# Linear ReLU attention on one core: K, V and Q prepared an octet ahead, first loads in whole rows, two stores cut by partitions

## The chip, the core and the metric

The kernel runs on one core of a Trainium2 chip. Its time is device microseconds (us), here of the one core. The profile comes from one profiled execution. The engines are PE (matmul) with its weight loads (PEld), DVE (vector), ACT (scalar), POOL (GpSimd) and SP (which only issues transfers). DMA transfers are issued by SP, ACT and POOL.

## The reference

```python
batch, heads, seq, dim = 8, 12, 512, 64          # Q, K, V: float32
Q_feat = np.maximum(0, Q)
K_feat = np.maximum(0, K)
KV = np.einsum('bhkd,bhkv->bhdv', K_feat, V)
K_sum = np.sum(K_feat, axis=2)
numerator = np.einsum('bhqd,bhdv->bhqv', Q_feat, KV)
denominator = np.einsum('bhqd,bhd->bhq', Q_feat, K_sum)
return (numerator / (denominator[:, :, :, None] + 1e-10)).astype(np.float32)
```

There are 96 heads of 512 rows of 64 numbers. Each of Q, K, V and the output is 12.58 MB of float32.

## The kernel before

Heads are taken in groups of four for K and V (24 groups `g`) and in octets of eight for Q and the output (12 octets `o`; octet `o` holds groups `2o` and `2o+1`). A tile has 128 partitions; a partition holds 16 consecutive rows of K or V (4 KB of float32) or 32 rows of Q or of the output (8 KB). So the 32 partitions of one head lie together.

**Loads.** Groups 0 and 1 are loaded as float32 by SP (K, L99) and ACT (V, L100), each tensor in two halves of 8 rows, 2 KB per partition. They borrow two buffers of the output pool (`kv_first`). Everything else is loaded by POOL, which turns float32 into bfloat16 on the way: Q of octet 0, and then per octet K, V, K, V, Q (`load_kv`, `load_q`; L85, L87, L91). All these loads are issued in program order from the start and run ahead as far as the pools (`kin` and `vin` 12 buffers, `qin` 7) and the outstanding transfers permit.

**Preparation of a group.** `prep` makes on DVE two copies of relu(K), one masked to the even heads and one to the odd (L130), and a copy of V masked to one half of the partitions (L132). `prep_act` makes on ACT the copy of V masked to the other half (L136). Beside V stands a column of ones, which yields the sum of K. The buffers are `kf` (pool `kfp`, 3) and `vo` (`NB`, 3).

**Products.** `mm_kv` makes 16 matmuls on PE (L141) that sum K times V over the rows of four heads. `evac_kv` copies the result by four ACT instructions into `kvd` (L148), laid out for two heads at a time.

**Q.** `transp` transposes Q by 16 matmuls with an identity, in two halves of eight (L155), and `evac_qt` takes the relu by two ACT instructions per half (L161) into `qtz` (two buffers).

**Output.** `mm_out` makes numerators and denominators of an octet in three rounds of 48, 48 and 32 matmuls (L176); `norm` adds 1e-10, takes the reciprocal and multiplies, on DVE (L186, L188, L189), into `o_sb`. `store` issues the transfer to HBM from SP (L204). Ahead of the store of each octet `o` below 7, SP reads a few bytes of K of octet `o+5` into `scratch` (L199). That read waits for the landing of that K, so it holds back the store, and all later ones, until loads five octets ahead have landed (`DELAY = 5`). The stores of octets 7 to 11 are issued in two halves of 16 rows, 4 KB per partition.

The order of all work is written out by hand; each engine takes its instructions in the order of the program. The loop runs over octets, and the outputs lag by one: pass `o` makes the products of group `2o`, prepares `2o+1`, makes two output rounds of octet `o-1`, the products of `2o+1`, the DVE part of the preparation of `2o+2`, the third round and the store of `o-1`, the transposes of Q of octet `o`, and at last `prep_act` of `2o+2`.

Of the kernel before, what the change touches and what calls it, by code (L numbers as in the profile page):

```python
# [10 lines left out]
def kernel(  # L11
# [7 lines left out]
    nc = tc.nc  # L19
    B, H, S, D = Q.shape  # L20
    assert D == 64
    P = 128
# [4 lines left out]
    R = S * 4 // P  # L27
    RQ = S * 8 // P
# [3 lines left out]
    NO = NG // 2  # L32
# [4 lines left out]
    fp32 = mybir.dt.float32  # L37
    bf16 = mybir.dt.bfloat16
    Act = mybir.ActivationFunctionType
    Alu = mybir.AluOpType  # L40

    def pool(name, bufs, **kw):
        return ctx.enter_context(tc.tile_pool(name=name, bufs=bufs, **kw))
# [2 lines left out]
    qin = pool("qin", 7)  # L46
    kin = pool("kin", 12)
    vin = pool("vin", 12)
    kfp = pool("kfp", 3)
    rcp = pool("rcp", 4)  # L50
    outp = pool("outp", DELAY + 2)
    pkv = pool("pkv", 2, space=bass.MemoryType.PSUM)
# [3 lines left out]
    def view(X, f):  # L56
        return X.rearrange("b h s d -> (b h s d)").rearrange("(n p f) -> n p f", p=P, f=f)

    Qr, Kr, Vr, Or = view(Q, RQ * D), view(K, R * D), view(V, R * D), view(out, RQ * D)

    ident = consts.tile([P, P], bf16, name="ident")
    NB = 3
    NK = 4
    NZ = 2

# [2 lines left out]

    vo = [consts.tile([P, R, 2, D1], bf16, name=f"vo{i}") for i in range(NB)]
    kvf = [consts.tile([P, NHG * 2 * D1], bf16, name=f"kvd{i}") for i in range(NK)]  # L70
# [6 lines left out]
    qtz = [x.rearrange("p z (u w y c) -> p z u w y c", u=U, w=4, y=2) for x in qtf]  # L77
# [3 lines left out]
    q_sb, k_sb, v_sb = {}, {}, {}  # L81
# [7 lines left out]
    def load_q(o):  # L89
        q_sb[o] = qin.tile([P, U, 2 * D], bf16, name="q_sb")  # L90
        nc.gpsimd.dma_start(out=q_sb[o].rearrange("p u f -> p (u f)"), in_=Qr[o])  # L91


    for g in range(F32):
        kv = outp.tile([P, 2, R, D], fp32, name="kv_first", tag="o_sb")
        k_sb[g], v_sb[g] = kv[:, 0], kv[:, 1]
        for i in range(2):
            rs, fs = slice(R // 2 * i, R // 2 * (i + 1)), slice(R // 2 * D * i, R // 2 * D * (i + 1))
            nc.sync.dma_start(out=k_sb[g][:, rs].rearrange("p r d -> p (r d)"), in_=Kr[g][:, fs])  # L99
            nc.scalar.dma_start(out=v_sb[g][:, rs].rearrange("p r d -> p (r d)"), in_=Vr[g][:, fs])  # L100
    load_q(0)
    make_identity(nc, ident)
    for o in range(1, NO):
# [4 lines left out]
    def zero(i):  # L108
        if i == 0:
            for h in range(NHG):  # L110
                for s in range(2):
                    nc.vector.memset(mask[32 * h:32 * h + 32, 0, s:s + 1], 1.0 if h % 2 == s else 0.0)
            for t in range(2):
                nc.vector.memset(mask[:, 1, t:t + 1], 0.0)
                nc.vector.memset(mask[64 * t:64 * t + 64, 1, t:t + 1], 1.0)
        if i < NB:
            nc.vector.memset(vo[i][:, :, :, D:D1], 0.0)
            for t in range(2):
                nc.vector.memset(vo[i][64 * t:64 * t + 64, :, t, D:D1], 1.0)
        nc.vector.memset(kvf[i].bitcast(fp32), 0.0)  # L120

    def zero_q(i):
        nc.vector.memset(qtf[i].rearrange("p z f -> p (z f)").bitcast(fp32), 0.0)  # L123
# [3 lines left out]
    def prep(g):  # L127
        kf[g] = kfp.tile([P, R, 2, D], bf16, name="kf")
        for s in range(2):
            nc.vector.tensor_scalar(kf[g][:, :, s, :], k_sb[g], scalar1=0.0,  # L130
                                    scalar2=mask[:, 0, s:s + 1], op0=Alu.max, op1=Alu.mult)
        nc.vector.tensor_scalar(vo[g % NB][:, :, 0, 0:D], v_sb[g], scalar1=mask[:, 1, 0:1],  # L132
                                scalar2=None, op0=Alu.mult)

    def prep_act(g):
        nc.scalar.activation(vo[g % NB][:, :, 1, 0:D], v_sb[g], Act.Copy, scale=mask[:, 1, 1:2])  # L136

    def mm_kv(g):
        ps_kv[g] = pkv.tile([P, 2, D1], fp32, name="ps_kv")
        for r in range(R):  # L140
            nc.tensor.matmul(  # L141
                ps_kv[g], kf[g][:, r, :, :].rearrange("p s d -> p (s d)"), vo[g % NB][:, r, :, :],
                start=(r == 0), stop=(r == R - 1), skip_group_check=True)

    def evac_kv(g):
        for s in range(2):
            for c in range(2):
                nc.scalar.copy(kvd[g % NK][64 * c:64 * c + 64, :, s, c, :],  # L148
                               ps_kv[g][64 * s:64 * s + 64])


    def transp(o, i):
        ps_qt[o, i] = pqt.tile([P, U // 2, P], bf16, name="ps_qt")
        for u in range(U // 2):
            nc.tensor.transpose(ps_qt[o, i][:, u, :], q_sb[o][:, i * (U // 2) + u, :], ident)  # L155

    def evac_qt(o, i):
        us = slice(i * (U // 2), (i + 1) * (U // 2))
        pv = ps_qt[o, i].rearrange("p u (w y c) -> p u w y c", w=4, y=2)
        for z in range(2):  # L160
            nc.scalar.activation(qtz[o % NZ][:, z, us, :, z, :], pv[:, :, :, z, :], Act.Relu)  # L161


    ROUNDS = ((0, 6), (6, 6), (12, 4))
# [1 line left out]
    def mm_out(o, j):  # L166
        po = pou.tile([P, 2, 512], fp32, name="ps_out")
        ps_out[o, j] = po
        u0, nu = ROUNDS[j]
        for v in range(nu):  # L170
            u, b, c = u0 + v, v // (nu // 2), v % (nu // 2) * 2 * D1
            for z in range(2):
                for w in range(4):
                    hs = slice(32 * w, 32 * w + 32)
                    h = 2 * w + z
                    nc.tensor.matmul(  # L176
                        po[hs, b, c:c + 2 * D1],
                        qtf[o % NZ][:, z, u * P + 32 * w:u * P + 32 * w + 32],
                        kvd[(2 * o + h // 4) % NK][:, h % 4 // 2, h % 2, :, :],
                        start=(z == 0), stop=(z == 1), skip_group_check=True)  # L180

    def norm(o, j, o_sb):
        u0, nu = ROUNDS[j]
        pv = ps_out[o, j][:, :, 0:nu * D1].rearrange("p b (r d) -> p b r d", d=D1)
        den = rcp.tile([P, 2, nu], fp32, name="den")
        nc.vector.tensor_scalar(den, pv[:, :, :, D], scalar1=1e-10, scalar2=None, op0=Alu.add)  # L186
        rec = rcp.tile([P, 2, nu], fp32, name="rec")
        nc.vector.reciprocal(rec, den)  # L188
        nc.vector.tensor_tensor(  # L189
            o_sb[:, 2 * u0:2 * (u0 + nu)].rearrange("p (b r) d -> p b r d", b=2),  # L190
            pv[:, :, :, 0:D],
            rec.unsqueeze(3).to_broadcast([P, 2, nu, D]), op=Alu.mult)

    def store(o, o_sb):
        if o + DELAY < NO:
            nc.sync.dma_start(out=scratch, in_=k_sb[2 * (o + DELAY)][0:1, 0, :])  # L199
        parts = 2 if o >= NO - 5 else 1  # L200
        n = RQ // parts
        for j in range(parts):
            rs = slice(n * j, n * (j + 1))
            nc.sync.dma_start(out=Or[o].rearrange("p (r d) -> p r d", d=D)[:, rs], in_=o_sb[:, rs])  # L204

    zero(0)
    prep(0)
    prep_act(0)
    zero(1)
    zero_q(0)  # L210
    o_sb = {}
    for o in range(NO + 1):
        if o < NO:
            mm_kv(2 * o)
            prep(2 * o + 1)
            prep_act(2 * o + 1)
            evac_kv(2 * o)
        if o == 0:
            for k in range(2, NK):
                zero(k)  # L220
            zero_q(1)
        if o > 0:
            o_sb[o - 1] = outp.tile([P, RQ, D], fp32, name="o_sb", tag="o_sb")
            for j in range(2):
                mm_out(o - 1, j)
                norm(o - 1, j, o_sb[o - 1])
        if o < NO:
            mm_kv(2 * o + 1)
            evac_kv(2 * o + 1)
        if o + 1 < NO:  # L230
            prep(2 * o + 2)
        if o > 0:
            mm_out(o - 1, 2)
            norm(o - 1, 2, o_sb[o - 1])
            store(o - 1, o_sb[o - 1])
        if o < NO:
            for i in range(2):
                transp(o, i)
                evac_qt(o, i)
        if o + 1 < NO:  # L240
            prep_act(2 * o + 2)
# [1 line left out]
_INS = ['Q', 'K', 'V']  # L243
_OUTS = [((8, 12, 512, 64), 'float32')]
# [25 lines left out]
```

## Time and profile before

| | us |
|---|---|
| median of 8 runs | 133.66 |
| lowest, highest | 131.95, 135.38 |
| the profiled execution | 133.41 |
| its span, first to last instruction | 131.6 |
| PE matmul busy | 78.7 |
| PE weight loads busy | 70.2 |
| DVE busy | 79.1 |
| ACT busy | 76.9 |
| POOL busy | 32.6 |

The profile numbers the lines as in the listing above. Its slices cut the span into 40 equal parts of 3.29 us, and each digit is a share in tenths. A share of the DMA engines is the time of the packets of all queues over 16 engines, so it can pass 1 where packets of two queues are under way on one engine together. q0 is the queue of POOL's loads, q1 that of SP, q10 that of ACT. A wait is put down to the instruction or the transfer that released it.

### The profile page before, as it was taken

The numbers are of one execution on the slowest core, as the hardware profiler recorded it, in microseconds if no ns is written. First come the engines' busy times: TensorE is split into PE (matmuls) and PEld (weight loads), VectorE is DVE, ScalarE is ACT, GpSimd is POOL, SyncE is SP. The second block draws the span as 40 slices with busy tenths as digits, with TensorE's granted clock in tenths as the row PEclk, the third lists the DMA queues.
The fourth block names the chain that finished last, engine by engine and source line by source line (L and its number), as shares of the span: only waits on it lengthen the run. The fifth ranks groups of instructions, "written<-read, shape, count | busy, mean of one in ns | idle before, by whom it ended". The sixth has DMA issues, their size and how long they took to land.

```text
span 131.6 us, 4834 instructions
## 1 busy us (share of the span) xinstructions
PE 78.7 (60%) x2112; PEld 70.2 (53%) x2112; DVE 79.1 (60%) x207; ACT 76.9 (58%) x169; POOL 32.6 (25%) x62
## 2 busy tenths in 40 slices
PE   0022283992937929438947839829839739389710
PEld 0032274882937828327937639629729638279510
DVE  2174883395592982860791973943955927908580
ACT  0060669359598297387198593594693694972600
POOL 6802525324343431240240240151230000000000
PEclk9999999999997799985699995995995999968996
DMA  3999999999999999999999999999999999992725
GB/s 103 307 272 275 216 205 214 209 209 215 207 218 205 218 259 312 214 261 313 212 250 332 213 244 331 210 213 326 252 213 326 248 238 376 405 390 118 315 97 230
DMA packets 11909, 32.82 MB, mean 249 GB/s; under 512 B 1520, under 2 KB 1520, under 8 KB 10992
## 3 DMA queue, kind: packets, MB, share of 16 engines
q0 software_dynamic: 8064, 17.83, 70.9%
q1 hardware_dynamic: 3248, 13.63, 26.2%
q10 hardware_dynamic: 576, 1.05, 2.4%
q8 instruction: 16, 0.26, 0.7%
q14 instruction: 5, 0.04, 0.1%
HBM read 37.75 MB, written 12.58 MB: 382 GB/s over the span
## 4 chain that ended last, share of the span: by engine, by line
PE 52%; ACT 23%; DMA 8%; issue 7%; DVE 4%; SPq 1%; ACTq 0%; DVEq 0%
PE ps_out L176 25%; PE ps_kv L141 23%; ACT qt L161 14%; ACT vo L136 9%; DMA kv_first<-in_K_dram 8%; PE ps_qt L155 5%; DVE o_sb L189 2%; SPq L99 1%; DVE kf L130 1%; ACT kvd L148 1%; DVE rec L188 1%; DVE vo L132 1%; ACTq L265 0%; DVE den L186 0%; ACTq L136 0%
## 5 line engine op out<-in xcount | busy, mean ns | idle before, releaser
L141 PE MATMUL ps_kv<-vo,kf 128*128 128x130 bf16 x384 | 32.5, 249 | 43.2 <-ACT vo L136 38.4
L141 PEld LDWEIGHTS <-kf 128*128 128x128 bf16 x384 | 28.6, 112 | 46.3 <-issue 28.3
L148 ACT CAST kvd<-ps_kv 64x130 bf16<-64x130 f32 x96 | 25.3, 263 | 32.8 <-PE ps_kv L141 31.3
L176 PE MATMUL ps_out<-kvd,qt 128*32 128x130 bf16 x1536 | 35.4, 260 | 3.6 <-issue 2.3
L176 PEld LDWEIGHTS <-qt 128*32 128x32 bf16 x1536 | 30.2, 117 | 7.4 <-issue 3.9
L189 DVE TENSOR_TENSOR o_sb<-ps_out,rec 128x768 f32<-128x768 f32 (+1 forms) x36 | 31.3, 868 | 1.4
L186 DVE TENSOR_SCALAR den<-ps_out 128x12 f32<-128x12 f32 (+1 forms) x36 | 5.8, 161 | 37.3 <-PE ps_out L176 37.3
L161 ACT ACTIVATE qt<-ps_qt 128x512 bf16<-128x512 bf16 x48 | 24.9, 602 | 3.4 <-PE ps_qt L155 2.9
L136 ACT ACTIVATE vo<-v_sb,mask 128x1024 bf16<-128x1024 bf16 x22 | 24.7, 1190 | 0.0
L85 POOL DMA_DIRECT2D k_sb<-in_K_dram x22 | 12.5, 570 | 35.5 <-DMA q_sb<-in_Q_dram 22.5
L130 DVE TENSOR_SCALAR kf<-k_sb,mask 128x1024 bf16<-128x1024 bf16 x44 | 19.2, 477 | 0.0
L87 POOL DMA_DIRECT2D v_sb<-in_V_dram x22 | 12.4, 562 | 21.3 <-DMA k_sb<-in_K_dram 10.8
L155 PE MATMUL ps_qt<-ident,q_sb 128*128 128x128 bf16 x192 | 14.0, 227 | 0.7 <-issue 0.6
L155 PEld LDWEIGHTS <-q_sb 128*128 128x128 bf16 x192 | 11.7, 102 | 2.1 <-issue 0.9
L132 DVE TENSOR_SCALAR vo<-v_sb,mask 128x1024 bf16<-128x1024 bf16 x22 | 10.5, 478 | 0.0
L91 POOL DMA_DIRECT2D q_sb<-in_Q_dram x12 | 7.2, 600 | 7.9 <-DMA v_sb<-in_V_dram 5.6
L188 DVE RECIPROCAL rec<-den 128x12 f32<-128x12 f32 (+1 forms) x36 | 7.9, 220 | 1.2
L130 DVE TENSOR_SCALAR kf<-kv_first,mask 128x1024 bf16<-128x1024 f32 x4 | 2.8, 750 | 5.8 <-DMA kv_first<-in_K_dram 5.8
L136 ACT ACTIVATE vo<-kv_first,mask 128x1024 bf16<-128x1024 f32 x2 | 2.4, 1178 | 4.7 <-DMA kv_first<-in_V_dram 4.7
L136 ACT ACT_TABLE_LOAD x1 | 1.3, 1283 | 6.4 <-DMA kv_first<-in_V_dram 6.4
L123 DVE MEMSET qt<- 128x2048 f32 x2 | 3.5, 1765 | 0.8 <-issue 0.8
L132 DVE TENSOR_SCALAR vo<-kv_first,mask 128x1024 bf16<-128x1024 f32 x2 | 1.5, 747 | 0.0
(12 smaller groups left out, 3.2 us busy)
## 6 DMA issues: line engine op xcount, KB each, us to landing
out_dram<-o_sb SPq DMA_DIRECT2D x7, 1024.0 KB, 8.7
q_sb<-in_Q_dram POOLq DMA_DIRECT2D x12, 512.0 KB, 15.4
k_sb<-in_K_dram POOLq DMA_DIRECT2D x22, 256.0 KB, 14.1
v_sb<-in_V_dram POOLq DMA_DIRECT2D x22, 256.0 KB, 13.2
out_dram<-o_sb SPq DMA_DIRECT2D x10, 512.0 KB, 7.7
kv_first<-in_V_dram ACTq DMA_DIRECT2D x4, 256.0 KB, 7.0
kv_first<-in_K_dram SPq DMA_DIRECT2D x4, 256.0 KB, 6.8
scratch<-k_sb SPq DMA_DIRECT2D x7, 0.1 KB, 5.0
```

The source lines that it names most:

```text
L85: nc.gpsimd.dma_start(out=k_sb[g].rearrange("p r d -> p (r d)"), in_=Kr[g])
L87: nc.gpsimd.dma_start(out=v_sb[g].rearrange("p r d -> p (r d)"), in_=Vr[g])
L130: nc.vector.tensor_scalar(kf[g][:, :, s, :], k_sb[g], scalar1=0.0, scalar2=mask[:, 0, s:s + 1], op0=Alu.max, op1=Alu.mult)
L132: nc.vector.tensor_scalar(vo[g % NB][:, :, 0, 0:D], v_sb[g], scalar1=mask[:, 1, 0:1], scalar2=None, op0=Alu.mult)
L136: nc.scalar.activation(vo[g % NB][:, :, 1, 0:D], v_sb[g], Act.Copy, scale=mask[:, 1, 1:2])
L141: nc.tensor.matmul(ps_kv[g], kf[g][:, r, :, :].rearrange("p s d -> p (s d)"), vo[g % NB][:, r, :, :], start=(r == 0), stop=(r == R - 1), s ...
L148: nc.scalar.copy(kvd[g % NK][64 * c:64 * c + 64, :, s, c, :], ps_kv[g][64 * s:64 * s + 64])
L155: nc.tensor.transpose(ps_qt[o, i][:, u, :], q_sb[o][:, i * (U // 2) + u, :], ident)
L161: nc.scalar.activation(qtz[o % NZ][:, z, us, :, z, :], pv[:, :, :, z, :], Act.Relu)
L176: nc.tensor.matmul(po[hs, b, c:c + 2 * D1], qtf[o % NZ][:, z, u * P + 32 * w:u * P + 32 * w + 32], kvd[(2 * o + h // 4) % NK][:, h % 4 // ...
L188: nc.vector.reciprocal(rec, den)
L189: nc.vector.tensor_tensor(o_sb[:, 2 * u0:2 * (u0 + nu)].rearrange("p (b r) d -> p b r d", b=2), pv[:, :, :, 0:D], rec.unsqueeze(3).to_broa ...
```

## The change

It has four parts. K and V of a group are prepared a whole octet before their products, with four buffers for `kf` and `vo` instead of three, and Q of octet `o` is transposed before the third output round of octet `o-1` rather than after it; the loop is written anew for that, with another order at its end. In the last octet the second half of the Q evacuation goes to DVE. The first loads of K and V are one transfer each, with 4 KB per partition. The stores of octets 1 and 3 are issued as five transfers of 112, 5, 5, 5 and 1 partitions, and those of octets 7 to 10 as one transfer instead of two halves.

```diff
-    kfp = pool("kfp", 3)
+    kfp = pool("kfp", 4)
...
-    NB = 3
+    NB = 4
...
-        for i in range(2):
-            rs, fs = slice(R // 2 * i, R // 2 * (i + 1)), slice(R // 2 * D * i, R // 2 * D * (i + 1))
-            nc.sync.dma_start(out=k_sb[g][:, rs].rearrange("p r d -> p (r d)"), in_=Kr[g][:, fs])
-            nc.scalar.dma_start(out=v_sb[g][:, rs].rearrange("p r d -> p (r d)"), in_=Vr[g][:, fs])
+        nc.sync.dma_start(out=k_sb[g].rearrange("p r d -> p (r d)"), in_=Kr[g])
+        nc.scalar.dma_start(out=v_sb[g].rearrange("p r d -> p (r d)"), in_=Vr[g])
...
-    def evac_qt(o, i):
+    def evac_qt(o, i, eng=None):
...
         for z in range(2):
-            nc.scalar.activation(qtz[o % NZ][:, z, us, :, z, :], pv[:, :, :, z, :], Act.Relu)
+            if eng is nc.vector:
+                eng.tensor_scalar(qtz[o % NZ][:, z, us, :, z, :], pv[:, :, :, z, :], scalar1=0.0,
+                                  scalar2=None, op0=Alu.max)
+            else:
+                nc.scalar.activation(qtz[o % NZ][:, z, us, :, z, :], pv[:, :, :, z, :], Act.Relu)
...
+    def cuts(o):
+        return ((16, P), (0, 5), (5, 10), (10, 15), (15, 16)) if o in (1, 3) else ((0, P),)
...
     def store(o, o_sb):
         if o + DELAY < NO:
             nc.sync.dma_start(out=scratch, in_=k_sb[2 * (o + DELAY)][0:1, 0, :])
-        parts = 2 if o >= NO - 5 else 1
-        n = RQ // parts
-        for j in range(parts):
-            rs = slice(n * j, n * (j + 1))
-            nc.sync.dma_start(out=Or[o].rearrange("p (r d) -> p r d", d=D)[:, rs], in_=o_sb[:, rs])
+        Ov = Or[o].rearrange("p (r d) -> p r d", d=D)
+        if o == NO - 1:
+            for j in range(2):
+                rs = slice(RQ // 2 * j, RQ // 2 * (j + 1))
+                nc.sync.dma_start(out=Ov[:, rs], in_=o_sb[:, rs])
+            return
+        for p0, p1 in cuts(o):
+            nc.sync.dma_start(out=Ov[p0:p1], in_=o_sb[p0:p1])

     zero(0)
     prep(0)
     prep_act(0)
     zero(1)
+    prep(1)
+    prep_act(1)
     zero_q(0)
-    o_sb = {}
+    for k in range(2, NK):
+        zero(k)
+    zero_q(1)
+    def kv(g):
+        mm_kv(g)
+        evac_kv(g)
+    def qt(o):
+        for i in range(2):
+            transp(o, i)
+            evac_qt(o, i, nc.vector if o == NO - 1 and i == 1 else None)
+    def prepare(g):
+        prep(g)
+        prep_act(g)
+    def out_round(o, j, o_sb):
+        mm_out(o, j)
+        norm(o, j, o_sb)
     for o in range(NO + 1):
-        if o < NO:
-            mm_kv(2 * o)
-            prep(2 * o + 1)
-            prep_act(2 * o + 1)
-            evac_kv(2 * o)
-        if o == 0:
-            for k in range(2, NK):
-                zero(k)
-            zero_q(1)
-        if o > 0:
-            o_sb[o - 1] = outp.tile([P, RQ, D], fp32, name="o_sb", tag="o_sb")
-            for j in range(2):
-                mm_out(o - 1, j)
-                norm(o - 1, j, o_sb[o - 1])
-        if o < NO:
-            mm_kv(2 * o + 1)
-            evac_kv(2 * o + 1)
-        if o + 1 < NO:
-            prep(2 * o + 2)
-        if o > 0:
-            mm_out(o - 1, 2)
-            norm(o - 1, 2, o_sb[o - 1])
-            store(o - 1, o_sb[o - 1])
-        if o < NO:
-            for i in range(2):
-                transp(o, i)
-                evac_qt(o, i)
-        if o + 1 < NO:
-            prep_act(2 * o + 2)
+        if o > 0:
+            o_sb = outp.tile([P, RQ, D], fp32, name="o_sb", tag="o_sb")
+        if o < NO - 1:
+            kv(2 * o)
+        if o > 0:
+            out_round(o - 1, 0, o_sb)
+        if o < NO - 2:
+            prepare(2 * o + 2)
+        if o > 0:
+            out_round(o - 1, 1, o_sb)
+        if o < NO - 1:
+            kv(2 * o + 1)
+            qt(o)
+        if o < NO - 2:
+            prepare(2 * o + 3)
+        if o > 0:
+            out_round(o - 1, 2, o_sb)
+            store(o - 1, o_sb)
+        if o == NO - 2:
+            prepare(2 * NO - 2)
+        if o == NO - 1:
+            prepare(2 * NO - 1)
+            kv(2 * NO - 2)
+            kv(2 * NO - 1)
+            qt(o)
```

## The prediction

> **What bounds the kernel now.** I read four views in this order: the page's slices and queue shares, the busy time by stretches, the waits, and the last part of the timeline with the landings of single transfers. First the page's head, its DMA rows and its queue shares:
>
> ```profile
> span 131.6 us, 4834 instructions
> ...
> PE 78.7 (60%) x2112; PEld 70.2 (53%) x2112; DVE 79.1 (60%) x207; ACT 76.9 (58%) x169; POOL 32.6 (25%) x62
> ...
> DMA  3999999999999999999999999999999999992725
> ...
> q0 software_dynamic: 8064, 17.83, 70.9%
> q1 hardware_dynamic: 3248, 13.63, 26.2%
> q10 hardware_dynamic: 576, 1.05, 2.4%
> ...
> HBM read 37.75 MB, written 12.58 MB: 382 GB/s over the span
> ```
>
> No engine is busy for more than 60%, but the DMA row is full from slice 1 to slice 35 and has holes only in the last four (118.5 us on). Busy time by stretches puts numbers on it (the last two columns are the DMA engines' share and GB/s written):
>
> ```profile
> 44.00:104.00 60.00, 41.12 (x1124) 36.76 (x1117) 38.72 (x98) 38.73 (x88) 15.47 (x27) 0.86 1.08 263
> 104.00:119.00 15.00, 9.29 (x268) 8.21 (x269) 8.26 (x22) 11.62 (x24) 0.00 (x0) 0.90 1.02 337
> 119.00:131.60 12.60, 5.91 (x232) 4.86 (x224) 7.03 (x17) 3.12 (x8) 0.00 (x0) 0.91 0.47 188
> ```
>
> A share over 1 means that packets of several queues lie on an engine at once: it is saturated. One octet moves 3 x 1.05 MB of fp32 in and 1.05 MB out, 4.19 MB; in steady state one octet's loads land every 10.0 us (the gate reads on SP, each released by a K load, start at 43.9, 53.9, 63.9, 73.9 us), that is 419 GB/s. Only at the end do the DMA engines run dry. The waits, however, show no steady-state compute instruction waiting for a load:
>
> ```profile
> PE ps_kv L141 <- ACT vo L136: 38.4, 12, 8.9
> DVE den L186 <- PE ps_out L176: 37.3, 13, 4.8
> ACT kvd L148 <- PE ps_kv L141: 31.3, 18, 3.1
> ...
> DVE kf L130 <- DMA kv_first<-in_K_dram: 5.8, 2, 3.6
> ```
>
> Compute waits on itself: PE for ACT's copy of V (L136), ACT and DVE for PE. So compute is late on its own account. The last Q load is issued at 97.06 us and lands 16.0 us later, at 113.1; its transposes begin at 121.38. The timeline of the end, PE and SP:
>
> ```profile
> 115.69 1.64 PE L141 MATMUL ps_kv<-vo,kf 128*128 128x130 bf16 x16 [2.76 <-ACT vo L136]
> 117.26 2.56 PE L176 MATMUL ps_out<-kvd,qt 128*32 128x130 bf16 x96
> 119.75 1.11 PE L141 MATMUL ps_kv<-vo,kf 128*128 128x130 bf16 x16
> 120.79 0.65 PE L176 MATMUL ps_out<-kvd,qt 128*32 128x130 bf16 x32
> 121.38 1.07 PE L155 MATMUL ps_qt<-ident,q_sb 128*128 128x128 bf16 x16
> ...
> 121.58 6.61 SPq L204 DMA_DIRECT2D out_dram<-o_sb  x4
> ```
>
> Octet 9's last store is issued at 114.35 and lands 7.2 us later, at 121.5; octet 10's first half is only issued at 121.58, octet 11's last at 127.86, landing at 130.75. Two limits in turn, then: DMA bandwidth until about 120 us, then a compute chain that is 8.3 us behind its loads (121.4 - 113.1) and feeds the last 2.1 MB of stores to idle DMA engines.
>
> **What the Trainium skill says.** "DMA: Bandwidth & Descriptors", Issuing engines are not separate DMA queues: transfers of all queues share the same 16 engines. The trace agrees: q0's share drops while q1 stores, and the sum stays near 1.08. The same page, Why a DMA increments its semaphore by 16: the engine count k is the largest up to 16 that divides the outer sizes, on the lowest-numbered engines. So 112 partitions give 7 rows to each of 16 engines, 5 partitions one row to engines 0 to 4, one partition one row to engine 0 unless it is split. No transfer here has such a shape, so the trace can't confirm it. "TensorE: Matmul & The Clock Gate", Part 1: an idle PE falls to half clock after about 3.4 us and needs as long to recover. The trace agrees in kind: clock 0.86 over 44 to 104 us, and 16 of L141's matmuls take 1.09 us or 1.89.
>
> **The change, part by part.** The sum is made on the profiled execution: span 131.6, time 133.41, so 1.8 us lie outside the span; the median of the runs, 133.66, is 0.25 above it.
>
> *Preparation and transposes ahead.* Instruction counts stay. Before, in each octet, the order is K and V copies, products, Q transposes, evacuation, and ACT's V copy (L136) stands behind four evacuations of 0.6 us (L161): the chain L155, L161, L136, L141 costs 2.5 to 2.8 us of PE time each octet (38.4 us in 12 waits, of which 8.9 is the start). After, L141's inputs are made a loop pass earlier and PE finds them ready. The period was (121.4 - 17.2)/11 = 9.5 us; per octet DVE and ACT are busy some 6.2 to 6.5 us (from 44 to 104 us: 38.7/6) and PE 6.9, so without the stall a period of 7 to 8 us is possible. The loads deliver one octet per 7.5 us before stores begin (Q lands at 19.4, 26.8, 35.2), then per 10. Compute catches up 8.3 us in a few octets and then waits for loads. That wait is what is late next: `prepare` stands between two output rounds on DVE, so rounds of octet o-1 queue behind K and V of octet o+1; those land within 6 us after Q of octet o, and stores wait for K five octets ahead, so nobody who matters waits for them. POOL's queue and the load order stay; loads are paced by bandwidth, not by buffers, so freeing buffers sooner gains nothing.
>
> *What the end becomes.* The two last octets' 2.1 MB now follow without a hole. Octet 9's store halves (4 KB rows) land 1.24 us apart (120.27, 121.51), so a whole octet costs the slowest engine 2.5 us: 121.5 + 2 x 2.5 = 126.5 for the last landing, if stores are issued in time. Are they? With K, V (22, 23) landed at 109.0 and Q at 113.1: `prepare(23)` on DVE behind octet 10's rounds to about 113.2, L141 1.1, transposes 1.07 (to 115.4), evacuations behind L148's four casts to 116.6 (half of them now on DVE beside ACT; a PSUM-source move of its size isn't in the trace, I bound it between ACT's 0.5 and 1.2 us for two and take 1.1), then three rounds at 1.35 on DVE: store halves at about 120.2 and 121.2. Octet 10's store is issued by 114. An unloaded half lands 2.7 to 2.9 us after issue, so the compute path would end at 124.1 at full clock, under 126.5. Half clock would add 0.8 for L141, 0.9 for the transposes and 0.6 for the first round: 126.4. Bandwidth sets the end, with little to spare.
>
> *First loads in 4 KB rows.* Four transfers instead of eight. q10's share, 2.4% of 16 x 131.6 us over 512 data rows, is 99 ns for 2 KB; q1's stores, after taking out 50 us for K's first loads, are 26.2% - 2.4% = 501 us over 12.58 MB, 163 ns for 4 KB. 512 rows of 4 KB x (198 - 163) / 16 engines = 1.1 us at most; queues overlap at the start (share 1.07), so between 0 and 1.1; I take 0.6. The second group should land earlier too (13.3 before), which pulls compute's start forward by 2 to 3 us; loads hide that.
>
> *Stores in cuts.* Octets 1 and 3: engines 5 to 15 write 7 rows instead of 8, engines 0 to 4 ten, engine 0 eleven. One 8 KB row is 2 x 163 = 0.33 us; two fewer are 0.65 on eleven engines, 1.3 to 2.0 more on five. A DMA ends with its slowest engine, and the engines are far apart: for the last Q load the trace has the first of its 16 completion marks at 108.0 and the last at 113.1. No view says which engine is late. Value: -0.65 if it is one of 5 to 15, +1.3 to +2.0 if one of 0 to 4; I take -0.6, eleven of sixteen and an early group of at least five being there to take the load. SP issues eight more transfers at 0.5 us, in the middle of 10 us of waiting. Whole stores for octets 7 to 10 have 8 KB rows instead of 4 KB: nothing, the rate is the same.
>
> *Sum.* 126.5 - 0.6 - 0.6 = 125.3; plus 0.85 from landing to span's end (131.6 - 130.75) = 126.2; I add 0.3 for holes between queues: 126.5. Plus 1.8 outside: 128.3 against 133.41. On the median's level: 128.4, or 3.9% faster.
>
> **Rivals.**
> A. The compute tail sets the end. If PE runs at half clock (for: PE now idles for loads, clock 0.57 from 116 to 120 even before; against: its last octet is dense), or if octet 10's rounds end later than I lay them, store halves come at 123.5 and 124.5: last landing 127.4, time about 130.5 with a late round.
> B. The cuts load the late engines: 128.4 + 0.6 + 1.3 to 2.0 = 130.5.
> C. The reordering doesn't speed compute, a new hand-over between DVE and PE taking L136's place (for: DVE rounds hold PSUM for PE, 37.3 us of waits; against: PE then has two more tasks to go on with). Only the start's gain remains: 132.5 to 134, no change.
> D. Slower: PE at half clock throughout. Then L141 costs 2 x 1.89, L176 2.72 + 1.2, L155 1.9: 9.6 us an octet, and with 0.2 of hand-over 9.8. It decides from a period of 9.6: starting 3 us earlier, the last transposes come at 14.2 + 11 x 9.8 = 122, the slow tail adds 10.2 + 2.3, and with 1.8 outside the time is 136. Against it: before, with PE no busier, the granted clock is 0.90.
>
> **How the numbers follow.** Forecast 0.66, A 0.17, B 0.06, C 0.06, D 0.05. About 1% is what a measurement of this kernel can tell from no change. Faster by over 1%: forecast, A and B, 0.89; within: C, 0.06; slower: D, 0.05. Low end: if the engines end level (the mean of the 16 completion marks of octet 9's last store is 119.7, not 121.5) and the start gives 1.1, the time is 126.3. High end: A and B with a margin, 131.2.
>
> **What would show it.** Right: the DMA row full to the last two slices; few holes after 119 us; DVE or ACT waiting for k_sb, v_sb and PE for q_sb loads; "PE ps_kv <- ACT vo" mostly gone; last Q landing near 112; a span near 126.5. For the first loads: group 1 landed by about 10.5 us. For the cuts: last Q completions closer than 5 us. Wrong: holes after the last Q landing with DMA share below 0.8 (A), a longer load phase (B), an unchanged 8 us between the last Q's landing and its transposes (C), or a mean clock below 0.7 (D).

## The result, and the profile after

The changed kernel takes 127.51 us (median of 11 runs, 127.36 to 127.72); the kernel before, run beside it and earlier, 133.93 (32 runs). The ratio is 0.964, with a 95% interval of 0.961 to 0.967; it compares the fast runs of each kernel alone (the kernel before runs from 131.17 to 135.38 us) and so lies nearer to 1 than the quotient of the medians, 0.952. The forecast was 128.4, 3.9% under the 133.66 that it started from; on that base 127.51 is 4.6% less. The profiled execution took 127.5 us and its span is 125.7.

First the page's head of the kernel after, with the rows shown of before:

```profile
span 125.7 us, 4876 instructions
...
PE 76.6 (61%) x2112; PEld 67.4 (54%) x2112; DVE 81.0 (64%) x212; ACT 76.5 (61%) x167; POOL 31.5 (25%) x62
...
DMA  3999999999999999999999999999999999999994
...
q0 software_dynamic: 8064, 17.83, 74.4%
q1 hardware_dynamic: 2416, 13.63, 27.1%
q10 hardware_dynamic: 288, 1.05, 2.2%
q8 instruction: 16, 0.26, 0.8%
...
HBM read 37.75 MB, written 12.58 MB: 400 GB/s over the span
```

The DMA row now has no hole before its last slice. The engines did the same work in nearly the same busy time (PE 76.6 us for 78.7, DVE 81.0 for 79.1); what is gone are the hollow slices at the end. Busy time by stretches (last two columns: DMA share and GB/s written):

```profile
44.00:104.00 60.00, 41.51 (x1204) 36.42 (x1203) 39.96 (x98) 42.00 (x95) 14.03 (x26) 0.89 1.09 262
104.00:119.00 15.00, 9.31 (x304) 8.12 (x304) 9.53 (x26) 7.11 (x16) 0.00 (x0) 0.89 1.04 360
119.00:125.70 6.70, 0.13 (x12) 0.00 (x0) 1.72 (x4) 0.00 (x0) 0.00 (x0) 0.71 0.69 281
```

After 119 us the DMA share is 0.69 where it was 0.47, and the stretch is 6.7 us long where it was 12.6. The middle moves data at the same rate as before. The waits:

```profile
PE ps_out L178 <- issue: 15.2, 9, 3.3
ACT vo L134 <- DMA v_sb<-in_V_dram: 9.6, 5, 3.9
PE ps_kv L139 <- ACT vo L134: 8.9, 2, 8.1
```

PE's wait for ACT's copy of V (38.4 us in 12 waits before) is down to 8.9 in two, 8.1 of it the start. ACT now waits for loads of V, as it never did in steady state before. And PE's wait "issue" before the output rounds, 2.3 us in two waits before, is 15.2 in nine: it stood still with nothing in this view that it waited for. More of that below. The end on PE and SP:

```profile
111.83 1.92 PE L139 MATMUL ps_kv<-vo,kf 128*128 128x130 bf16 x16 [2.24 <-DVE vo L130]
113.53 1.77 PE L153 MATMUL ps_qt<-ident,q_sb 128*128 128x128 bf16 x16
...
116.12 1.52 PE L178 MATMUL ps_out<-kvd,qt 128*32 128x130 bf16 x92 [0.25 <-ACT qt L163]
...
119.78 1.47 SPq L211 DMA_DIRECT2D out_dram<-o_sb  x2
```

The last Q load is issued at 95.54 us and lands 16.0 later, at 111.5; its transposes begin at 113.5. Compute's lag behind its loads has shrunk from 8.3 us to 2.0. The last two store halves are issued at 119.8 and 120.8 and land at 123.6 and 124.8, 3.8 and 4.0 us after issue; in the kernel before, on idle engines, they took 2.6 and 2.9. The stores queue: the engines set the end, by some 1.1 us.

### The profile page after: what moved, and what is told of

It is laid out like the page before. It is cut to its first block, busy times and chain, and to the rows that moved or that the text cites. A ratio compares the mean times of both kernels' runs of the same rounds, so it can differ in the third digit from the quotient of the medians.

```text
span 125.7 us, 4876 instructions
## 1 busy us (share of the span) xinstructions
PE 76.6 (61%) x2112; PEld 67.4 (54%) x2112; DVE 81.0 (64%) x212; ACT 76.5 (61%) x167; POOL 31.5 (25%) x62
## 3 DMA queue, kind: packets, MB, share of 16 engines
q10 hardware_dynamic: 288, 1.05, 2.2%
## 4 chain that ended last, share of the span: by engine, by line
DMA 32%; PE 30%; issue 14%; DVE 12%; ACT 7%; ACTq 1%; SPq 0%
DMA v_sb<-in_V_dram 25%; PE ps_out L178 14%; PE ps_kv L139 12%; DMA kv_first<-in_K_dram 7%; PE ps_qt L153 3%; ACT kvd L146 3%; DVE o_sb L191 3%; DVE qt L121 3%; ACT qt L163 3%; DVE kf L128 2%; DVE vo L130 2%; ACT vo L134 1%; DVE rec L190 1%; ACTq L294 0%; DVE den L188 0%
## 5 line engine op out<-in xcount | busy, mean ns | idle before, releaser
L178 PE MATMUL ps_out<-kvd,qt 128*32 128x130 bf16 x1536 | 32.8, 238 | 18.9 <-issue 15.2
L139 PEld LDWEIGHTS <-kf 128*128 128x128 bf16 x384 | 27.3, 111 | 24.4 <-DVE vo L130 16.4
L178 PEld LDWEIGHTS <-qt 128*32 128x32 bf16 x1536 | 26.1, 105 | 24.3 <-issue 17.6
L134 ACT ACTIVATE vo<-v_sb,mask 128x1024 bf16<-128x1024 bf16 x22 | 26.1, 1188 | 9.7 <-DMA v_sb<-in_V_dram 9.6
L163 ACT ACTIVATE qt<-ps_qt 128x512 bf16<-128x512 bf16 x46 | 23.9, 602 | 0.5 <-PE ps_qt L153 0.2
L153 PE MATMUL ps_qt<-ident,q_sb 128*128 128x128 bf16 x192 | 16.1, 249 | 2.7 <-issue 2.7
L153 PEld LDWEIGHTS <-q_sb 128*128 128x128 bf16 x192 | 14.5, 115 | 2.8 <-issue 2.8
L91 POOL DMA_DIRECT2D q_sb<-in_Q_dram x12 | 6.5, 542 | 8.4 <-DMA v_sb<-in_V_dram 4.5
L160 DVE TENSOR_SCALAR qt<-ps_qt 128x512 bf16<-128x512 bf16 x2 | 0.8, 418 | 3.6 <-PE ps_qt L153 3.6
```

What stands on the lines that cost most here:

```text
L139: nc.tensor.matmul(ps_kv[g], kf[g][:, r, :, :].rearrange("p s d -> p (s d)"), vo[g % NB][:, r, :, :], start=(r == 0), stop=(r == R - 1), s ...
L178: nc.tensor.matmul(po[hs, b, c:c + 2 * D1], qtf[o % NZ][:, z, u * P + 32 * w:u * P + 32 * w + 32], kvd[(2 * o + h // 4) % NK][:, h % 4 // ...
```

## The experiments

### Two cuts, no cuts, three, five

Edits of the cut function alone:

```diff
 e1_no_cuts
-        return (...five cuts...) if o in (1, 3) else ((0, P),)
+        return ((0, P),)
 e11_three_cuts
+        return (...five cuts...) if o in (1, 3, 5) else ((0, P),)
 e9_five_cuts
+        return (...five cuts...) if o in (0, 1, 2, 3, 4) else ((0, P),)
```

> The changed kernel with the stores of octets 1 and 3 as one transfer each. Theory (the DMA engines set the end and the latest of them are among 5 to 15): each of those gets two 8 KB rows back, 2 x 0.33 us; 127.5 + 0.4 to 0.65 = 127.9 to 128.2, and the last Q load's 16 completion marks spread wider again than the 4.4 us of the changed kernel. Rival 1 (the compute tail sets the end): 127.5. Rival 2 (a late engine is among 0 to 4 and the cuts cost time): 126.5 to 127.0.

> The changed kernel with the stores of octets 1, 3 and 5 cut, three instead of two. Theory (two cuts nearly level the engines, whose last marks lie 1.2 us apart): the eleven win 0.33, the five lose 0.65 and engine 0 1.0; 127.4 to 128.2. Rival (the eleven are still late by more than a row): 127.2.

> The changed kernel with the stores of octets 0 to 4 cut, five instead of two: against two cuts, engines 5 to 15 write three 8 KB rows less (-1.0 us each), engines 0 to 4 six more (+2.0), engine 0 nine more (+2.9). Theory (the five lowest engines were the early ones by about 1.5 to 2.3 us, as the marks without cuts lie apart, and two cuts nearly level them): now these five are late, 124.8 for the last landing becomes about 126 to 127: 128.7 to 129.7. Rival (any row taken from engines 5 to 15 still helps): 127.0 or less. Rival (the engines that get the rows are not the early ones, or the cut only changes something in the middle): 127.5.

Measured: none 128.13 us (127.92 to 128.31), two 127.51 (127.36 to 127.72), three 128.45 (128.29 to 128.59), five 130.45 (130.37 to 130.72). Two cuts bring 0.62, which fits the two rows of 0.33 that eleven engines write less (an 8 KB packet of q1 took 0.32). The expected wider spread for the last Q load without cuts did not show: its marks go from 107.5 to 111.6, 4.1 us, against 4.4. What the cuts moved shows in octet 10's store, which is issued while the engines are full. Without cuts its 16 completion marks fall into two halves, eight at 119.8 to 121.2 us and eight at 122.0 to 122.8. With two cuts three stay early (119.3 to 120.0) and thirteen lie together, at 121.5 to 122.3. The traces of e8_three_buffers and e10_shifted_pe, with two cuts, have the same three and thirteen; that of e3_order_only, with none, the same two halves.

The marks also show how many engines a transfer uses. One of 112 partitions leaves 16. One of 5 partitions leaves five about 8 us after its issue, and one of 1 partition a single one; each has besides a mark half a microsecond after the issue, too early for a landing. So five engines take part in the one and one engine in the other: the single row is not split.

From the third cut on, time rises, and by more than was expected: 0.94 for one more, 2.94 for three more. In the profiled executions the last landing moves from 124.78 us (two cuts) to 125.27 (three) and 127.29 (five). From three to five that is 1.01 per cut: three rows of 0.33 and not the two that engines 0 to 4 have in common. From two to three it is only 0.49; the rest of that execution's 0.82 comes after the last landing. So with five cuts one engine that takes all three small transfers and the single row is the last. Its mark stands alone, 0.5 us after the one before it, where with three cuts the last four marks lie within 0.15 us. By the rule of the Trainium skill ("DMA: Bandwidth & Descriptors", Why a DMA increments its semaphore by 16) that is engine 0; the profile does not name engines. With five cuts the last stretches, DMA share in the column before the last, show the few engines left:

```profile
125.00:126.00 1.00, 0.00 (x0) 0.00 (x0) 0.00 (x0) 0.00 (x0) 0.00 (x0) 0.50 0.41 168
126.00:126.50 0.50, 0.00 (x0) 0.00 (x0) 0.00 (x0) 0.00 (x0) 0.00 (x0) 0.50 0.14 57
126.50:127.00 0.50, 0.00 (x0) 0.00 (x0) 0.00 (x0) 0.00 (x0) 0.00 (x0) 0.50 0.04 16
```

One engine of 16 is a share of 0.06: from 126 us on two are at work on average, from 126.5 on less than one. Two cuts are the best of the four numbers tried.

### First loads in halves, with and without the cuts

```diff
 e2_half_first: K and V of groups 0 and 1
-        nc.sync.dma_start(out=k_sb[g].rearrange(...), in_=Kr[g])
-        nc.scalar.dma_start(out=v_sb[g].rearrange(...), in_=Vr[g])
+        for i in range(2):
+            ...
+            nc.sync.dma_start(out=k_sb[g][:, rs].rearrange(...), in_=Kr[g][:, fs])
+            nc.scalar.dma_start(out=v_sb[g][:, rs].rearrange(...), in_=Vr[g][:, fs])
 e3_order_only: the same, and no cuts
```

> The changed kernel with each first load of K and V in two halves with 2 KB per partition. Theory: the engines lose time in the first 8 us that is never made good, since they are full until the end. In the two profiles Q of octet 1 lands at 19.35 and 18.04, so +1.3: 128.8. By the prediction's own term, +0.6: 128.1. Rival (the start is hidden by later slack): 127.5.

> The changed kernel with both of the two other parts undone: stores of octets 1 and 3 whole, first loads in halves. What is left is the new order of the work with four buffers (and whole stores for octets 7 to 10). Theory: the order closes the holes at the end, 133.9 to about 129.3, and the two other parts add what they add alone. Rival (the parts need each other, for instance compute must start earlier to catch up): over 130.5.

Measured: 129.21 us (128.53 to 130.12) and 129.14 (128.87 to 129.24), against before 0.970 (0.962 to 0.977) and 0.968 (0.962 to 0.974). So what is left in the second brings most of the gain: 0.968 of the whole change's 0.964, in medians 134.02 to 129.14. That is the new order together with the whole stores of octets 7 to 10 and the last evacuation's half on DVE; no run takes these apart. Whole first rows bring 1.0 without cuts (128.13 against 129.14) and 1.7 with them (129.21 against 127.51), more than any theory had. The cuts bring nothing while the first loads are in halves. The end of the kernel with halves and cuts says why:

```profile
115.75 1.47 PE L155 MATMUL ps_qt<-ident,q_sb 128*128 128x128 bf16 x16
117.81 0.30 PE L180 MATMUL ps_out<-kvd,qt 128*32 128x130 bf16 x4 [0.58 <-ACT qt L165]
118.30 2.68 PE L180 MATMUL ps_out<-kvd,qt 128*32 128x130 bf16 x92 [0.19 <-ACT qt L165]
121.21 1.06 PE L180 MATMUL ps_out<-kvd,qt 128*32 128x130 bf16 x32 [0.24 <-DVE o_sb L193]
...
122.52 1.37 SPq L213 DMA_DIRECT2D out_dram<-o_sb  x2
```

The last store halves are issued at 122.5 and 123.6 and land 2.6 and 2.9 us later, on idle engines: the compute tail sets this end. PE runs it at half clock (2.68 us for 92 matmuls, 1.52 in the changed kernel), and its transposes start 2.2 us later though the last Q lands at 112.1, only 0.6 later. Those 0.6 are the DMA cost of the halves, seen also in octet 10's store (122.9 against 122.3). The rest is compute: with halves, transposes of octet 0 begin at 16.9 us and not at 14.0, and that delay is never wholly made good.

### The old order with the new loads and stores

> The kernel before with the new first loads and the new stores (cuts, whole stores for octets 7 to 10), the order of the work as before. Theory: the compute chain sets the end, so the 0.4 to 0.65 of the cuts is lost, and of the loads only the earlier start of compute remains (the second K group lands at 10.2 and not 13.3): 131 to 133. Rival (what counts is DMA time, wherever it is saved): 133.9 - 1.3 - 0.5 = 132.1 with the DMA row full to the end; rival (loads and cuts carry the gain): below 130.

The edit takes the loop and the buffers of before, and the loads and the stores of after. Measured: 131.88 us (130.72 to 134.19), 0.987 of before (0.978 to 0.995). The end is hollow as before, here in a stretch of its profiled execution, which at 134.19 us is the longest of the seven:

```profile
119.00:132.40 13.40, 6.35 (x244) 5.31 (x236) 7.27 (x18) 3.12 (x8) 0.00 (x0) 0.88 0.40 161
```

A share of 0.40 in the last 13 us: DMA time saved is lost here. Rival "DMA time counts wherever it is saved" came as near in time (132.1), but asked for a row that is full to the end. That the gain is that of an earlier start of compute is not shown. In this execution the transposes of octet 0 do begin earlier (14.3 us, in the kernel before 17.2), but those of octet 11 do not (121.8 and 121.4), and it gained nothing.

### One store less

```diff
     def store(o, o_sb):
+        if o == 2:      # e5, e7; o == 8 in e6
+            return
```

> The changed kernel without the store of octet 2 (and its gate read): 1.05 MB less to move in the middle. Theory (DMA bandwidth sets the end): 1.05 MB / 419 GB/s = 2.5 us off, 125.0. Rival (compute or a fixed latency sets the end): 127.5; rival (the compute tail is close behind): a gain of 1 or less.

> The changed kernel without the store of octet 8, which is among the last transfers, after the loads. Theory: DMA time falls by 2.5 us but the last loads land no earlier, so the last store halves are still issued at 119.8 and 120.8 and land unhindered 2.8 us later, at 123.6 and not 124.8: only 1.1 off, 126.4. That measures the room between the DMA limit and the compute tail. Rival (no compute limit near): 125.0.

> The kernel before without the store of octet 2. Theory (its compute chain sets the end, the engines only wait): 133.9, no change. Rival (DMA bandwidth sets the end of this one too): 131.4.

In the kernel before, 1.05 MB less to move changes little: ratio 0.995 (0.990 to 1.000), where a DMA limit asked for 0.981. So bandwidth did not set its end. The changed kernel gains about 1.5 us in both cases: 125.99 (four runs, 125.42 to 127.32) without store 2 and 125.97 (125.85 to 126.86) without store 8. For store 8 that is what the theory said, within 0.4: the last halves land 2.6 and 2.9 us after issue, at 123.2. For store 2 the theory asked for 2.5 and got 1.5. The profiled execution is the longest of the four, 127.32, and gained only 0.2. In it the last Q load lands at 109.0, 2.5 earlier as it should, but its transposes begin 5.4 us after it and not 2.0: there compute didn't follow. For the other three, which gained 1.3 to 2.1, no trace shows what stopped them. So bandwidth sets the end of the changed kernel, with compute some 1.5 us behind it. The run e10_shifted_pe, shown below, says the same from the other side: its last store halves are issued 1.9 and 1.7 us earlier than in the changed kernel, and land within 0.1 us of the same times.

### Three buffers

> The changed kernel with three buffers for kf and for vo, as before, in place of four. Theory (three suffice for the new order, since the products of a group are made before the buffer is wanted again, and compute has slack anyway): 127.5. Rival (the fourth buffer is needed for the preparation to run ahead): PE waits for L134 again and 129 or more.

```diff
-    kfp = pool("kfp", 4)
+    kfp = pool("kfp", 3)
-    NB = 4
+    NB = 3
```

Measured: 127.53 us (127.42 to 127.62). The fourth buffers do nothing.

### What PE waits for

In the kernel after, PE stands still every so often. The timeline of PE, around octet 4 and 5:

```profile
48.78 0.28 PE L178 MATMUL ps_out<-kvd,qt 128*32 128x130 bf16 x5
51.87 0.47 PE L178 MATMUL ps_out<-kvd,qt 128*32 128x130 bf16 x19 [2.80 <-issue]
52.27 1.11 PE L139 MATMUL ps_kv<-vo,kf 128*128 128x130 bf16 x16
53.31 1.52 PE L178 MATMUL ps_out<-kvd,qt 128*32 128x130 bf16 x92
58.16 0.30 PE L178 MATMUL ps_out<-kvd,qt 128*32 128x130 bf16 x4 [3.33 <-issue]
```

Most pauses fall in the midst of rounds that PE has begun. Between these two it makes 19 + 16 + 92 = 127 matmuls. Two tests, of one execution each; the second leaves out the loads of octets 6 to 11:

```diff
 e10_shifted_pe, ahead of all other PE work
+    ps_warm = pqt.tile([P, U // 2, P], bf16, name="ps_qt")
+    for x in range(32):
+        nc.tensor.transpose(ps_warm[:, x % 8, :], ident, ident)
 e12_loads_stop
     for o in range(1, NO):
+        if o >= 6:
+            for g in (2 * o, 2 * o + 1):
+                k_sb[g], v_sb[g] = k_sb[g - 10], v_sb[g - 10]
+            q_sb[o] = q_sb[o - 6]
+            continue
```

> The changed kernel with 32 transposes of the identity ahead of PE's first product, while PE waits for its first loads anyway; their output is never read. In the changed kernel PE stands still without a releaser (1.2 to 3.3 us, 'issue') before matmuls 223, 351, 606, 734, 861, 1117, 1244, 1372, 1627 and 1882 of its stream: all about 95 more than a multiple of 127.7. Theory (PE waits for the next 16 KB of its own instructions, which hold 128 weight loads and 128 matmuls): counted from the stream's start, with the 32, the pauses stay at the same numbers, so 32 matmuls earlier in the work. Rival (a hand-over in the work, a semaphore that the profile does not show): they stay at the same work, so at numbers 32 higher. The time is 127.5 in both.

> The changed kernel without the loads of octets 6 to 11: their K, V and Q are those of earlier octets, still in their buffers, so about from 50 us on the DMA engines carry stores alone. Theory (PE's pauses are instruction fetches that queue behind data on full DMA engines): with the engines partly idle the pauses go (under 0.5 us each after 60 us) and the period of an octet falls from 8.9 to 7 to 8 us: end at about 105. Rival (PE needs the pauses by itself, whatever the engines do): 1.2 to 3.3 us each 128 matmuls as before, a period of 8.5 or more.

With 32 more matmuls ahead, the pauses of over 1 us stay at the same places of the stream (before matmuls 351, 606, 734, 861, 1244 and 1372 again, and at 989 too) and so move in the work:

```profile
46.15 0.93 PE L139 MATMUL ps_kv<-vo,kf 128*128 128x130 bf16 x13
50.08 0.35 PE L139 MATMUL ps_kv<-vo,kf 128*128 128x130 bf16 x3 [3.00 <-issue]
50.27 1.05 PE L153 MATMUL ps_qt<-ident,q_sb 128*128 128x128 bf16 x16
51.25 0.65 PE L178 MATMUL ps_out<-kvd,qt 128*32 128x130 bf16 x32
```

The pause that stood after 13 of the 32 matmuls of a third round now stands before the last 3 products: 3 + 16 + 13 = 32 matmuls earlier. A hand-over in the work would not have moved. Of the other four numbers named, 1117 and 1882 have shorter pauses (0.8 and 0.4 us), 223 and 1627 next to none; at numbers 32 higher there is none at all. The time is 127.45.

Without the loads of octets 6 to 11 the pauses end with the full engines. The last long one ends at 51.3 us. In the same 30 us, this kernel first and then the changed one:

```profile
60.00:90.00 30.00, 25.62 (x824) 22.08 (x824) 26.77 (x69) 28.70 (x67) 0.00 (x0) 1.00 0.46 184
```

```profile
60.00:90.00 30.00, 23.04 (x665) 20.17 (x667) 20.51 (x52) 23.16 (x51) 7.99 (x15) 0.88 1.09 260
```

With a DMA share of 0.46 PE makes 824 matmuls instead of 665, at full clock, and ACT is busy 96% of the time. An octet takes 6.5 us (transposes at 62.1, 68.7, 74.8, 81.3, 87.8), and the time is 110.45, where 7 to 8 and about 105 had been expected. From 60 us on PE waits 0.6 us for "issue" in all; the changed kernel, from 60 to 108, 5.6 us in the rounds alone. The loads that it lacks would also have held it up, so its speed is not PE's alone; but the pauses in mid-round hang on full engines.

The Trainium skill ("Runtime: NRT & Kernel Launch", Terms) says that an engine's instruction memory is refilled in 16 KiB blocks. The page's q8 row agrees, with 16 packets of 16 KB in the span; 128 weight loads and 128 matmuls to a block are then 64 bytes each. That the pauses come once per 127 or 128 matmuls, stay with the stream and vanish when the engines have room is shown.

The packets themselves decide it. Each of the 16 lasts 0.9 to 1.0 us, and the trace has its time. The pause that ends at 58.16 us has one in its midst; the queue shares of the stretch from 55.8 to 56.8 us have it whole, 5.6% of 16 engines' time:

```profile
q8 instruction: 1, 0.02, 5.6%
```

It ends at 56.8, and PE goes on 1.4 us later. So it is each time: the ten pauses of the changed kernel, the seven of over 1 us with 32 matmuls ahead and the one of the kernel before (55.75 us) all end 1.2 to 1.6 us after a packet of q8 has ended. From 25 to 112 us the packets start 5.9 to 6.8 us apart, 6.2 on average; without the later loads, from 57 to 83 us, 3.6 to 4.8. An estimate from these: 128 matmuls in 6.2 us are 8.5 us for an octet's 176. What stays open is when a packet is asked for: that it waits in the engines' queues, rather than being asked for late, is not shown.

## Why the prediction was right, point by point

**Two limits in turn.** Right. Without a store the kernel before does not gain, and the changed one does. The old order throws away DMA time (share 0.40 at its end).

**The end.** Right, nearly to the time of each step: store halves were laid at 120.2 and 121.2 and came at 119.8 and 120.8; the last landing was put at 125.3 and came at 124.8; the span at 126.5 and came at 125.7. PE did run the last products and transposes at half clock, 1.92 and 1.77 us, 1.5 more than in the sum, but DVE had finished octet 10 and the last preparation 1.4 earlier than laid, at 111.8. That these two cancel in the times of the store halves is luck; the landing does not hang on it. The two last octets' stores land 2.5 us apart (119.8, 122.3, 124.8), as set. The 0.3 for holes between queues was not needed. A slip in the sum's last line changes little: 128.3 and 0.25 are 128.55, not 128.4.

**The cuts.** -0.6 was set, 0.62 measured. It was a guess which engines are late, eleven chances in sixteen by the prediction's own words, and it came out. The early group was there: eight of the 16 marks of octet 10's store without cuts. But the room was narrow: "an early group of at least five being there to take the load" was true for two cuts and no longer for the third. The sign named for the cuts, last Q completions closer than 5 us, tells nothing: without cuts they are 4.1 apart. Rival B's direction is what three and five cuts show.

**The first loads.** Here a term was mis-sized: -0.6 was set, and 1.7 measured with the cuts (1.0 without), enough for the 0.9 us by which the time came in under the forecast. The DMA part is about as set: octet 10's store lands 0.6 us earlier with whole rows, 0.7 where there are no cuts (123.5 and 122.8). The step that failed is "pulls compute's start forward by 2 to 3 us; loads hide that". They hide it only when compute has caught up, and with halves it hadn't.

**Catching up.** "A period of 7 to 8 us is possible", and "catches up 8.3 us in a few octets": wrong. From octet 1 to 11 the transposes are (113.5 - 24.4)/10 = 8.9 us apart, 0.4 less than the 9.3 of before over the same octets, and the lag falls to near nothing only at octet 9 (transposes 0.2 us after landing). The sum didn't see PE's pauses for its own instructions, which take the place of ACT's V copy in part: packets 6.2 us apart allow, by the estimate above, no less than about 8.5 us for an octet on average. That is rival C's mechanism in a milder form and with another cause than "a new hand-over between DVE and PE".

**Rival A**, the compute tail, did not happen in the changed kernel, but with the first loads in halves it did, at 129.2 us, half clock included. It was near.

**The fourth buffers** had no term, and need none.

## What to carry to other kernels

Where the transfers are full to the end but for the last slices, look which chain feeds those last transfers: bringing it forward gains only until the transfers are full to the end. A part that saves DMA time is worth nothing under the wrong limit (the cuts with a late start: nothing; with an early one: 0.6), so parts have to be measured on top of the one that moves the limit. When transfers end with their slowest engine, rows can be moved from late engines to early ones, but the optimum is narrow: one step too many cost more (0.94 us) than the two steps had gained (0.62). When PE stops in the midst of a round with no releaser, count the matmuls between its pauses and look when the packets of q8 come.

## What the runs showed of the hardware

PE pauses of 1.2 to 3.3 us without a releaser, once per 127 or 128 matmuls at most, come with full DMA engines, end 1.2 to 1.6 us after a 16 KB packet of its instructions has landed, and go when the engines have room. In the kernel before they are nearly hidden (one of 1.9 us, ending at 55.75) under PE's waits for ACT. PE's program is thus a user of the DMA engines: with a pair of weight load and matmul per 128 bytes of instructions, this kernel of short matmuls, which also fills the engines, has PE fed late.

The 16 engines do not keep step: for one transfer (the last Q load of the kernel before) the first and the last completion marks lie 5 us apart, and a few rows of 8 KB (0.33 us each) are enough to shift the end.

A store of 5 partitions used five engines and one of 1 partition one, by their completion marks; stores of 112 and 128 partitions used 16.
